# Low-rank scaling and key rotation moved into the attention, and the w_up block sums spread over 18 of its 24 items

## The chip, the cores and the metric

The kernel runs on one core of one Trainium2 chip. The metric is the device time of one execution in microseconds (us), given as the median of three runs. Of the core's engines, PE (TensorE) multiplies matrices, DVE (VectorE), ACT (ScalarE) and POOL (GpSimd) work element by element, and SP only issues DMAs. POOL issues DMAs too; these are the only ones here that add to their destination.

## The reference

Two layers, each with a mixer of three parts that read one normalised input, then a memory cross-attention and a gated feed-forward network (FFN). What the change touches is the mixer's latent attention and the weights of the FFN:

```python
c_q, c_kv, k_rope, g_q, g_k, g_v, g_m = jnp.split(z, offs, axis=-1)          # 256, 128, 32 columns, ...
qa  = (rms_norm(c_q, mla_q_norm) @ mla_w_uq).reshape(B, S, MLA_HEADS, MLA_NOPE + MLA_ROPE)
kva = (rms_norm(c_kv, mla_kv_norm) @ mla_w_ukv).reshape(B, S, MLA_HEADS, MLA_NOPE + MLA_V)
k_pe = apply_rope(k_rope.reshape(B, S, 1, MLA_ROPE), *rope_a)
...
y_a = block_attention(q_a, k_a, v_a, (MLA_NOPE + MLA_ROPE) ** -0.5)          # 6 heads
y_b = block_attention(q_b, k_b, v_b, GQA_DIM ** -0.5)                        # 6 heads
...
a = h @ w_up                                                                 # 1024 x 5632, in the FFN
```

All is float32, with 1024 tokens and a width of 1024.

## The kernel before

A float32 product is made of three products of rounded halves (`mm3`, lines 115 to 118: hi·hi, hi·lo, lo·hi). So each operand is split: ACT writes the rounded half (lines 123 and 126), DVE the rest (lines 124 and 127).

The FFN multiplies 2 x 2 blocks by a seven-product scheme, which needs sums of blocks of `w_up`. They are made in DRAM while the attention runs: the class `Blocks` cuts `w_up` into 24 steps per layer (`steps`). Each step is a copy from DRAM to DRAM (`copy`, line 778, issued by SP) and later an adding DMA onto the copy (`add`, line 783, issued by POOL). Most of them move 1 MB. The sums of `w_down` have 12 copies in the same stretch; their adds come in the FFN.

The attention (`attention`) runs over 24 items, 12 of six heads with 64 columns (`gqa`), then 12 of the latent heads (`mla`), each item one head and half of the queries. An item has four steps: PE makes 1024 scores per row (lines 726 and 727 or `mm3`), DVE takes their maximum (line 295), ACT the exponentials (line 299), DVE the reciprocal of their sum (line 304) and POOL scales the row (line 305). Five steps later PE transposes the rows (line 140), ACT and DVE split them, and PE multiplies them with the values (lines 318 and 319); ACT and POOL put the two halves of a result together (lines 326 to 328).

Between the steps the attention runs what the lists `fill[item]` hold. `q_cols` (`fill[0]` and `fill[1]`) makes the latent queries from the transposed low-rank columns `cqT` (made by `turn_cq`) and the halves of `w_uq`; `rope_q(h)` (`fill[8 + 2h]`) rotates a head's queries: two DVE products (lines 236, 238), two POOL products (lines 237, 239), two DVE sums (lines 240, 241). `y_squares` adds squares on POOL (line 664). What `extra[item]` holds is run at the third step of an item: there stand the copies and adds.

Just ahead of the attention, the loop over `w_a` makes the low-rank columns in eight token tiles. Behind tiles 3 and 7 it scales a half of them by the reciprocal root of their mean squares (lines 551 to 556: two small DVE instructions, one on POOL, and two DVE products of 1024 and 512 columns). Behind the loop stands the rotation of the key columns `kr` (`rope`).

All this is recorded in program order, and a scheduler then sets each engine's order. Engines run their own queue in order and wait for each other by semaphores. The issue of an add is an entry of POOL's queue like any other, so what stands behind it waits for it.

The two lines that place a step n of 24 are:

```python
g = n * 14 // len(steps)
extra.setdefault(g + 4, []).append(lambda w=w, m=m, i=i: w.add(m, i))
```

Of the kernel before, what the change touches and what calls it, by code (L numbers as in the profile page):

```python
# [8 lines left out]
F32 = mybir.dt.float32  # L9
F32R = mybir.dt.float32r  # L10
AF = mybir.ActivationFunctionType
ALU = mybir.AluOpType
AX = mybir.AxisListType

P = 128
# [4 lines left out]
CH = 512  # L20
NC = S // CH
TPC = CH // P
# [47 lines left out]
def trunk(ctx: ExitStack, tc: tile.TileContext, a: dict, out: bass.AP):  # L70
# [16 lines left out]
    def stat():  # L87
        return stats.tile([P, 16], F32, tag="stat", name="stat")
# [7 lines left out]
    def v3(ap, b):  # L96
        return ap.rearrange("p (a b) -> p a b", b=b)
# [286 lines left out]
    def layer(l, nt, w_m, last):  # L384
# [129 lines left out]
        def turn_q(j, c):  # L514
# [7 lines left out]
            if c == 1:  # L522
                sl.put(zq[j])

        cq = [sl.get(F32) for _ in range(2)]
        ckv = sl.get(F32)
        kr = lpool.tile([P, NT * ROPE], F32, tag="kr", name="kr")
        for t in range(NT):
            b = proj(t, w_a, 416, 2)
            c, tt = divmod(t, TPC)  # L530
            if tt == 0:
                ssq = stat()
            junk = sl.get(F32)
            nc.scalar.activation(junk[:, :256], b[:, :256], AF.Square, accum_out=ssq[:, tt : tt + 1])
            nc.scalar.activation(junk[:, :P], b[:, 256:384], AF.Square, accum_out=ssq[:, 4 + tt : 5 + tt])
            sl.put(junk)
            nc.scalar.activation(cq[c][:, tt * 256 : (tt + 1) * 256], b[:, :256], AF.Copy)
            nc.scalar.activation(ckv[:, t * P : (t + 1) * P], b[:, 256:384], AF.Copy)
            nc.scalar.activation(kr[:, t * ROPE : (t + 1) * ROPE], b[:, 384:416], AF.Copy)
            if t == 0:  # L540
                qn_ = [head_norm(z, tab[:, T_GQ : T_GQ + 64], tab) for z in zq]
            for j, st in Q_STEPS[t]:
                qn_[j][st]()
            if t == 5:
                tc.keep_in_program_order(nc.scalar.activation(stat()[:, 0:1], mhalf[:, 0:1], AF.Exp))
            if t == 6:
                turn_q(0, 0)
                turn_q(0, 1)
            if tt == TPC - 1:
                v, r = stat(), stat()  # L550
                nc.vector.tensor_scalar(v[:, 0:4], ssq[:, 0:4], 1.0 / 256, EPS, ALU.mult, ALU.add)
                nc.vector.tensor_scalar(v[:, 4:8], ssq[:, 4:8], 1.0 / P, EPS, ALU.mult, ALU.add)
                nc.gpsimd.tensor_tensor(r[:, :8], v[:, :8], mhalf[:, :8], ALU.pow)
                for z, n, o in ((cq[c], 256, 0), (ckv[:, c * CH : (c + 1) * CH], P, 4)):
                    z = v3(z, n)
                    nc.vector.tensor_tensor(z, z, r[:, o : o + 4].unsqueeze(2).to_broadcast([P, TPC, n]), ALU.mult)
        put2(w_a)
        nt.free()
        w_uq = [load(a["w_uq"][l, k], 576, True) for k in range(2)]
        w_ukv = load(a["w_ukv"][l], 768, True)  # L560
        cos3, sin3 = v3(tab[:, T_COSA : T_COSA + P], 16), v3(tab[:, T_SINA : T_SINA + P], 16)
        tmp = sl.get(F32)
        rope(kr.rearrange("p (t i two) -> p t i two", i=16, two=2), cos3, sin3, [v3(tmp[:, o * P : (o + 1) * P], 16) for o in range(4)])
        sl.put(tmp)


        cqT, ckvT, kT, qn, vm, qT, yT = [None] * 2, [None], [None] * 3, [None] * MLA_H, {}, {}, [None] * KT
# [229 lines left out]

        items = [gqa(h, c) for h in range(GQA_H) for c in range(NC)]
        items += [mla(h, c) for h in range(MLA_H) for c in range(NC)]
        fill[0] += [lambda k=k: turn_cq(0, k) for k in range(2)]  # L800
        fill[1] += [lambda k=k: turn_cq(1, k) for k in range(2)]
        for t in range(NT):
            fill[t // 4] += [lambda t=t: q_cols(t, 0), lambda t=t: q_cols(t, 1)]
# [46 lines left out]

        extra, steps = {}, w_u.steps()
        for n, (w, m, i) in enumerate(steps):
            g = n * 14 // len(steps)
            extra.setdefault(g, []).append(lambda w=w, m=m, i=i: w.copy(m, i))
            extra.setdefault(g + 4, []).append(lambda w=w, m=m, i=i: w.add(m, i))
        later = deque(sorted(w_d.steps(), key=lambda s: (5, 7, 6, 3).index(s[1])))
        for n, (w, m, i) in enumerate(later):
            extra.setdefault(n * 20 // len(later), []).append(lambda w=w, m=m, i=i: w.copy(m, i))
# [624 lines left out]
```

## Time and profile before

| what | us |
|---|---|
| median of three runs (2798.71 to 2804.17) | 2800.31 |
| the profiled execution | 2792.72 |
| its span, first to last instruction | 2790.7 |
| PE busy in the span | 2732.1 |
| DVE, ACT, POOL busy | 1966.8, 1469.7, 688.0 |

The profile is of one execution. A row of its timeline is: start in us, length in us, engine, line, operation, what is written and read, and in brackets how long the engine had been idle before and what is taken to have released it. "PEclk" or "granted clock" is the share of TensorE's full clock.

### The profile page before, as it was taken

The page shows a single profiled execution, that of the slowest core. Times are in us where ns is not written, and L with a number is a line of the kernel's source. Part 1 is how long each engine was busy: PE and PEld are TensorE (multiplying, and loading weights), DVE is VectorE, ACT ScalarE, POOL GpSimd, SP SyncE. Part 2 cuts the span into 40 slices and gives each one's busy share as a digit, 9 for nine tenths or more (in the row PEclk, how much of TensorE's full clock was granted, in tenths as well). Part 3 has the DMA queues.
Part 4 walks back from the last instruction along what each step waited for, and adds up shares of the span by engine and source line. Part 5 has one row for each costly group of instructions (what it writes and reads, how often), then busy time and mean ns, then how long its engine had stood idle before and what let it go on. Part 6 is the DMA issues. An engine that isn't in the chain of part 4 may idle for free.

```text
span 2790.7 us, 37974 instructions
## 1 busy us (share of the span) xinstructions
PE 2732.1 (98%) x13648; PEld 2289.4 (82%) x13648; DVE 1966.8 (70%) x2953; ACT 1469.7 (53%) x2838; POOL 688.0 (25%) x696
## 2 busy tenths in 40 slices
PE   9999999999999999999999999999999999999998
PEld 7987778888878888888889877788888788888887
DVE  5489889666697777774445798895566877777754
ACT  4368878324564444553333788782245544446442
POOL 3245666320001100000123355653200011100000
PEclk9999999999999999999999999999999999999999
DMA  4028991221149876785210389912211698757752
GB/s 145 27 80 229 264 243 38 79 65 48 65 138 237 227 211 169 223 270 185 86 59 21 108 244 251 226 39 68 69 61 46 165 242 221 205 173 233 257 184 104
DMA packets 160748, 418.80 MB, mean 150 GB/s; under 512 B 17840, under 2 KB 18480, under 8 KB 146224
## 3 DMA queue, kind: packets, MB, share of 16 engines
q1 hardware_dynamic: 137376, 323.84, 34.3%
q0 software_dynamic: 23040, 92.28, 18.1%
q8 instruction: 107, 1.75, 0.2%
q14 instruction: 81, 0.66, 0.1%
q10 hardware_dynamic: 144, 0.26, 0.0%
HBM read 371.75 MB, written 206.05 MB: 207 GB/s over the span
## 4 chain that ended last, share of the span: by engine, by line
PE 84%; DVE 6%; ACT 4%; issue 2%; POOL 2%; DMA 1%; SPq 0%; POOLq 0%; DVEq 0%; ACTq 0%
PE bank L1237 8%; PE bank L116 7%; PE bank L118 7%; PE bank L117 7%; PE pair L1237 6%; PE bank L140 6%; PE bank L1125 5%; PE bank L1126 5%; PE bank L1124 5%; PE pair L1124 4%; PE pair L1125 4%; PE pair L1126 4%; PE pair L116 2%; PE pair L118 2%; PE pair L117 2%; PE bank L319 2%
## 5 line engine op out<-in xcount | busy, mean ns | idle before, releaser
L116 PE MATMUL bank<-s,s 128*128 128x512 f32 (+4 forms) x1124 | 405.1, 360 | 5.6 <-DVE s L124 3.8
L124 DVE TENSOR_TENSOR s<-bank,s 128x512 fp32r<-128x512 f32 (+3 forms) x552 | 330.8, 630 | 106.1 <-ACT s L123 103.4
L118 PE MATMUL bank<-s,s 128*128 128x512 f32 (+4 forms) x1124 | 400.0, 357 | 5.4 <-DVE s L127 4.2
L117 PE MATMUL bank<-s,s 128*128 128x512 f32 (+4 forms) x1124 | 399.0, 355 | 0.3 <-DVE s L111 0.3
L123 ACT ACTIVATE s<-bank 128x512 fp32r<-128x512 f32 (+3 forms) x552 | 286.3, 556 | 208.9 <-PE bank L140 138.0
L140 PE MATMUL bank<-ident,s 128*128 128x128 f32 (+1 forms) x2320 | 327.8, 275 | 22.8 <-ACT s L327 6.4
L140 PEld LDWEIGHTS bank<-ident,s 128*128 128x128 f32 (+1 forms) x2320 | 272.4, 140 | 84.2 <-ACT s L327 12.2
L1077 ACT ACTIVATE s<-s 128x512 fp32r<-128x512 f32 x308 | 187.4, 627 | 181.5 <-PE bank L1126 46.6
L305 POOL TENSOR_SCALAR s<-s,stat 128x1024 f32<-128x1024 f32 x192 | 224.5, 1176 | 217.1 <-DVE stat L304 152.9
L1125 PE MATMUL bank<-s,s 128*128 128x512 f32 x704 | 274.5, 390 | 0.9 <-DVE s L209 0.9
L1126 PE MATMUL bank<-s,s 128*128 128x512 f32 x704 | 273.9, 389 | 0.0
L1124 PE MATMUL bank<-s,s 128*128 128x512 f32 x704 | 273.8, 389 | 0.0
L295 DVE TENSOR_REDUCE stat<-pair 128x1 f32<-128x1024 f32 x192 | 233.8, 1218 | 45.9 <-PE pair L727 27.1
L1237 PE MATMUL bank<-s,s 128*128 128x512 f32 (+1 forms) x1068 | 242.6, 387 | 1.6 <-DVE stat L131 1.6
L116 PEld LDWEIGHTS bank<-s,s 128*128 128x128 f32 x1124 | 212.4, 189 | 33.9 <-DVE s L124 5.6
L132 POOL TENSOR_TENSOR stat<-stat,mhalf 128x1 f32<-128x1 f32 (+3 forms) x94 | 82.2, 875 | 634.7 <-DVE stat L131 633.1
L118 PEld LDWEIGHTS bank<-s,s 128*128 128x128 f32 x1124 | 212.3, 189 | 31.1 <-DVE s L127 5.1
L1222 DVE TENSOR_TENSOR s<-s,s 128x512 fp32r<-128x512 f32 x264 | 170.8, 686 | 93.5 <-ACT s L1221 93.5
L1237 PEld LDWEIGHTS bank<-s,s 128*128 128x128 f32 x1068 | 198.7, 188 | 42.3 <-DVE x L1328 1.8
L117 PEld LDWEIGHTS bank<-s,s 128*128 128x128 f32 x1124 | 212.6, 189 | 23.8 <-DVE s L111 0.6
L299 ACT ACTIVATE s<-pair,stat 128x1024 f32<-128x1024 f32 x192 | 214.9, 1119 | 26.1 <-DVE stat L295 22.1
L1221 ACT ACTIVATE s<-s 128x512 fp32r<-128x512 f32 x264 | 153.7, 623 | 141.8 <-DMA s<-g_u 49.6
(182 smaller groups left out, 5529.2 us busy)
## 6 DMA issues: line engine op xcount, KB each, us to landing
s<-u SPq DMA_DIRECT2D x176, 256.0 KB, 4.2
u<-in_w_up SPq DMA_DIRECT2D x40, 1024.0 KB, 17.9
s<-in_w_up SPq DMA_DIRECT2D x132, 256.0 KB, 4.4
g_u<-s SPq DMA_DIRECT2D x88, 256.0 KB, 2.8
s<-g_u SPq DMA_DIRECT2D x88, 256.0 KB, 3.2
s<-d SPq DMA_DIRECT2D x88, 256.0 KB, 3.5
u<-in_w_up POOLq DMA_DIRECT2D x20, 1024.0 KB, 21.1
u<-u POOLq DMA_DIRECT2D x20, 1024.0 KB, 15.9
```

The lines of the kernel that those rows point to most:

```text
L116: nc.tensor.matmul(o, l[0], r[0], start=first, stop=False)
L117: nc.tensor.matmul(o, l[0], r[1], start=False, stop=False)
L118: nc.tensor.matmul(o, l[1], r[0], start=False, stop=last)
L123: nc.scalar.activation(hi, src, AF.Copy)
L124: nc.vector.tensor_tensor(lo, src, f(hi), ALU.subtract)
L140: nc.tensor.transpose(b[:m, j * P : (j + 1) * P], s, ident)
L295: nc.vector.reduce_max(self.nm[:, 0:1], s, axis=AX.X, negate=True)
L305: Item.last = nc.gpsimd.tensor_scalar(p, p, r[:, 0:1], 0.0, ALU.mult, ALU.add)
L1124: nc.tensor.matmul(o, lh, rh, start=k == 0 and m in (1, 5, 6), stop=False, skip_group_check=True)
L1125: nc.tensor.matmul(o, lh, rl, start=False, stop=False, skip_group_check=True)
L1126: nc.tensor.matmul(o, ll, rh, start=False, stop=k == 3, skip_group_check=True)
L1237: nc.tensor.matmul(o, lh[p], rh[q], start=m in (1, 5, 2) and i == 0 and k == 0, stop=i == NP - 1 and k == 2, skip_group_check=True)
```

## The change

It does three things. The scaling of the low-rank columns becomes a function `norm_low`; its second call (tiles 4 to 7) moves from the end of the projection to `fill[0]`, behind the transposes of the first half. The rotation of the keys becomes `rope_k` and moves to `fill[4]`. The 24 steps of `w_up` are put on 18 items in place of 14, and each add three items behind its copy in place of four: copies in items 0 to 17 in place of 0 to 13, adds in items 3 to 20 in place of 4 to 17. What is computed stays the same.

```diff
+        def norm_low(c, ssq):
+            v, r = stat(), stat()
+            nc.vector.tensor_scalar(v[:, 0:4], ssq[:, 0:4], 1.0 / 256, EPS, ALU.mult, ALU.add)
+            nc.vector.tensor_scalar(v[:, 4:8], ssq[:, 4:8], 1.0 / P, EPS, ALU.mult, ALU.add)
+            nc.gpsimd.tensor_tensor(r[:, :8], v[:, :8], mhalf[:, :8], ALU.pow)
+            for z, n, o in ((cq[c], 256, 0), (ckv[:, c * CH : (c + 1) * CH], P, 4)):
+                z = v3(z, n)
+                nc.vector.tensor_tensor(z, z, r[:, o : o + 4].unsqueeze(2).to_broadcast([P, TPC, n]), ALU.mult)
...
-            if tt == TPC - 1:
...
+            if t == TPC - 1:
+                norm_low(0, ssq)
...
-        tmp = sl.get(F32)
-        rope(kr.rearrange("p (t i two) -> p t i two", i=16, two=2), cos3, sin3, [v3(tmp[:, o * P : (o + 1) * P], 16) for o in range(4)])
-        sl.put(tmp)
+
+        def rope_k():
+            tmp = sl.get(F32)
+            rope(kr.rearrange("p (t i two) -> p t i two", i=16, two=2), cos3, sin3, [v3(tmp[:, o * P : (o + 1) * P], 16) for o in range(4)])
+            sl.put(tmp)
...
-        fill[0] += [lambda k=k: turn_cq(0, k) for k in range(2)]
+        fill[0] += [lambda k=k: turn_cq(0, k) for k in range(2)] + [lambda: norm_low(1, ssq)]
+        fill[4] += [rope_k]
...
-            g = n * 14 // len(steps)
+            g = n * 18 // len(steps)
             extra.setdefault(g, []).append(lambda w=w, m=m, i=i: w.copy(m, i))
-            extra.setdefault(g + 4, []).append(lambda w=w, m=m, i=i: w.add(m, i))
+            extra.setdefault(g + 3, []).append(lambda w=w, m=m, i=i: w.add(m, i))
```

The diff does not show what the scheduler makes of it. The rows below are of the built programs, in each engine's own order; "waits" are the engines whose semaphores an instruction waits for. The added lines move line numbers: 551 to 556 become 527 to 532, 664 becomes 669, 783 becomes 788.

DVE at the start of the first layer's attention, before: the second scaling (lines 551, 552, 556) and the rotation of `kr` (236 to 241) stand between the first maximum (295) and the two splits of the transposed low-rank columns (127, of the banks), for which PE's `q_cols` waits.

```order
L551 TENSOR_SCALAR stat<-stat 128x4 [waits Activation_49]
L552 TENSOR_SCALAR stat<-stat 128x4 [waits Activation_49]
L295 TENSOR_REDUCE stat<-pair 128x1 [waits PE_49]
L556 TENSOR_TENSOR s_102_1255<-s_102_1255,stat 128x1024 [waits Activation_49,Pool_49]
L556 TENSOR_TENSOR s_103_1256<-s_103_1256,stat 128x512 [waits Activation_49]
L236 TENSOR_TENSOR s_132_1616<-kr,s_73_703 128x128 [waits Activation_49]
L111 TENSOR_TENSOR s_128_1606<-s_126_1604,s_127_1605 128x576 [waits DMAHW7_49,DVE_49,Activation_49]
L238 TENSOR_TENSOR s_132_1616<-kr,s_73_703 128x128
L127 SCALAR_TENSOR_TENSOR s_135_1670<-bank,cols_86,s_134_1669 128x512 [waits PE_49]
L240 TENSOR_TENSOR kr<-s_132_1616 128x128 [waits DVE_49,Pool_49]
L241 TENSOR_TENSOR kr<-s_132_1616 128x128 [waits Pool_49]
L127 SCALAR_TENSOR_TENSOR s_137_1679<-bank,cols_86,s_136_1678 128x512 [waits PE_49]
```

The same place in the changed kernel:

```order
L295 TENSOR_REDUCE stat<-pair 128x1 [waits PE_49]
L127 SCALAR_TENSOR_TENSOR s_134_1656<-bank,cols_86,s_133_1655 128x512 [waits Activation_49]
L127 SCALAR_TENSOR_TENSOR s_136_1665<-bank,cols_86,s_135_1664 128x512 [waits Activation_49]
L527 TENSOR_SCALAR stat<-stat 128x4
L528 TENSOR_SCALAR stat<-stat 128x4
L295 TENSOR_REDUCE stat<-pair 128x1 [waits PE_49]
L111 TENSOR_TENSOR s_128_1599<-s_126_1597,s_127_1598 128x576 [waits DMAHW7_49,DVE_49,Activation_49]
L532 TENSOR_TENSOR s_102_1255<-s_102_1255,stat 128x1024 [waits Pool_49]
L532 TENSOR_TENSOR s_103_1256<-s_103_1256,stat 128x512
```

The two splits now stand right behind the first maximum, and the scaling behind them, with the second maximum ahead of its products; the rotation is gone from here.

POOL around the rotation of the fourth latent head (item 14), before: two adds in a row, then row scalings (305), a sum of squares (664) and the rotation's two products.

```order
L783 DMA u_5_4_1627<-in_w_up 128x2048 [waits DMAHW6_49]
L783 DMA u_5_5_1628<-in_w_up 128x2048 [waits DMAHW7_49]
L305 TENSOR_SCALAR s_340_3884<-s_340_3884,stat 128x1024 [waits DVE_49,Activation_49]
L664 TENSOR_TENSOR s_318_3683<-s_318_3683,s_344_3936 128x1024
L305 TENSOR_SCALAR s_343_3930<-s_343_3930,stat 128x1024 [waits DVE_49,PE_49]
L237 TENSOR_TENSOR s_348_3974<-s_142_1712,s_73_703 128x128 [waits PE_49]
L239 TENSOR_TENSOR s_348_3974<-s_142_1712,s_73_703 128x128
```

The same place in the changed kernel:

```order
L788 DMA u_3_2_1629<-u_6_2_1617 128x2048 [waits DMAHW4_49,DMASW6_49,DMASW3_49]
L305 TENSOR_SCALAR s_340_3877<-s_340_3877,stat 128x1024 [waits DVE_49,Activation_49]
L669 TENSOR_TENSOR s_318_3676<-s_318_3676,s_344_3928 128x1024 [waits Activation_49]
L237 TENSOR_TENSOR s_348_3966<-s_141_1705,s_73_703 128x128 [waits PE_49]
L239 TENSOR_TENSOR s_348_3966<-s_141_1705,s_73_703 128x128
L305 TENSOR_SCALAR s_343_3922<-s_343_3922,stat 128x1024 [waits DVE_49]
```

One add stands there in place of two, an earlier one in the order of the steps (5_4 and 5_5 now come some twenty entries later), and the rotation's products stand directly behind the sum of squares.

DVE at the place that the rotation of `kr` is moved to, some three items into the attention, in the changed kernel (before, lines 124, 295 and 304 follow each other here without it):

```order
L304 RECIPROCAL stat<-stat 128x1 [waits Activation_49]
L124 TENSOR_TENSOR s_189_2345<-bank,s_189_2345 128x512 [waits DVE_49,Activation_49]
L124 TENSOR_TENSOR s_190_2353<-bank,s_190_2353 128x512 [waits DVE_49,Activation_49]
L236 TENSOR_TENSOR s_192_2362<-kr,s_73_703 128x128 [waits DVE_49]
L238 TENSOR_TENSOR s_192_2362<-kr,s_73_703 128x128
L295 TENSOR_REDUCE stat<-pair 128x1 [waits PE_49]
L240 TENSOR_TENSOR kr<-s_192_2362 128x128 [waits DVE_49,Pool_49]
L241 TENSOR_TENSOR kr<-s_192_2362 128x128 [waits Pool_49]
```

The four DVE instructions of the rotation now stand between splits and maxima of the attention, where POOL is scaling rows. The second layer has the same orders.

## Rows read from the trace of the kernel before

**Rows 1.** Page, part 1: busy us, share of span, instructions of each engine.
```profile
PE 2732.1 (98%) x13648; PEld 2289.4 (82%) x13648; DVE 1966.8 (70%) x2953; ACT 1469.7 (53%) x2838; POOL 688.0 (25%) x696
```
**Rows 2.** Timeline, DVE, start of the first layer's attention: start, length, engine, line.
```profile
166.03 1.23 DVE L295 TENSOR_REDUCE stat<-pair 128x1 f32<-128x1024 f32 x1
167.74 2.35 DVE L556 TENSOR_TENSOR s<-s,stat 128x1024 f32<-128x1024 f32 x2 [0.49 <-POOL stat L553]
...
170.22 0.74 DVE L111 TENSOR_TENSOR s<-s,s 128x576 fp32r<-128x576 f32 x1
...
171.09 0.74 DVE L127 SCALAR_TENSOR_TENSOR s<-bank,cols,s 128x512 fp32r<-128x512 f32 x1
```
**Rows 3.** Timeline, PE: at this start, and near the end of the rotations.
```profile
171.88 0.40 PE L118 MATMUL bank<-s,s 128*128 128x288 f32 x1 [2.11 <-DVE s L127]
...
412.16 0.63 PE L140 MATMUL bank<-ident,s 128*128 128x128 f32 x4 [0.97 <-DVE s L124]
```
**Rows 4.** Timeline, POOL, in three stretches (both layers), around adds (L783).
```profile
299.73 0.81 POOL L783 DMA_DIRECT2D u<-in_w_up  x1 [3.87 <-DVE s L124]
300.29 2.50 POOL L305 TENSOR_SCALAR s<-s,stat 128x1024 f32<-128x1024 f32 x2
302.48 0.73 POOL L237 TENSOR_TENSOR s<-s,s 128x128 f32<-128x128 f32 x1
...
357.02 0.81 POOL L783 DMA_DIRECT2D u<-in_w_up  x1 [2.44 <-DVE s L124]
...
358.68 2.67 POOL L664 TENSOR_TENSOR s<-s,s 128x1024 f32<-128x1024 f32 x1
...
1741.13 0.84 POOL L783 DMA_DIRECT2D u<-in_w_up  x1 [4.17 <-DVE stat L304]
```
**Rows 5.** DMA issues by line at 285.0 and at 340.6 us: KB, us to landing.
```profile
u<-u POOLq DMA_DIRECT2D x1, 1024.0 KB, 14.4
...
u<-in_w_up SPq DMA_DIRECT2D x1, 1024.0 KB, 43.9
```
**Rows 6.** Timeline, DVE and PE, in the same three stretches.
```profile
300.59 3.20 DVE L236 TENSOR_TENSOR s<-s,s 128x128 f32<-128x128 f32 x1
...
305.78 0.50 PE L319 MATMUL bank<-s,s 128*128 128x512 f32 x1 [2.13 <-DVE s L124]
...
359.83 3.60 DVE L236 TENSOR_TENSOR s<-s,s 128x128 f32<-128x128 f32 x1
...
366.55 0.66 PE L140 MATMUL bank<-ident,s 128*128 128x128 f32 x4 [2.66 <-ACT s L327]
...
1742.22 5.34 DVE L236 TENSOR_TENSOR s<-s,s 128x128 f32<-128x128 f32 x1
...
1746.61 0.44 PE L140 MATMUL bank<-ident,s 128*128 128x128 f32 x2 [1.26 <-POOL s L305]
...
1750.66 0.98 PE L140 MATMUL bank<-ident,s 128*128 128x128 f32 x4 [2.92 <-ACT s L327]
```
**Rows 7.** Line L236: count, duration ns min/median/max, first and last start.
```profile
L236 DVE TENSOR_TENSOR s<-s,s x12: 274/926/5337, 272.3 to 1795.3; 128x128 f32<-128x128 f32 x12
```
**Rows 8.** Windows: us, busy PE, PEld, DVE, ACT, POOL, granted clock, DMA share, GB/s.
```profile
307.00:310.40 3.40, 3.40 (x12) 2.75 (x12) 2.67 (x4) 3.29 (x7) 1.45 (x2) 0.50 1.05 260
1556.40:1559.60 3.20, 3.20 (x15) 3.20 (x14) 2.20 (x4) 2.64 (x13) 1.16 (x2) 0.50 0.00 0
...
175.00:232.00 57.00, 56.30 (x348) 47.95 (x347) 45.92 (x78) 51.74 (x129) 24.34 (x23) 1.00 0.43 144
232.00:425.00 193.00, 181.12 (x1010) 146.22 (x1009) 167.94 (x290) 157.03 (x317) 118.24 (x116) 0.99 1.00 252
```
**Rows 9.** DMA queues from 232 to 425 us: packets, MB, share of 16 engines.
```profile
q0 software_dynamic: 3456, 23.07, 61.8%
q1 hardware_dynamic: 3600, 25.43, 37.7%
```
**Rows 10.** Line L295 in 160 to 560 us: duration ns, first and last start.
```profile
L295 DVE TENSOR_REDUCE stat<-pair x96: 1199/1215/1226, 166.0 to 501.6; 128x1 f32<-128x1024 f32 x96
```

More of the change, by code (lines that the diff above doesn't have):

```diff
@@ L548, in layer @@
                 turn_q(0, 1)
-            if tt == TPC - 1:
[L550 to L556, printed above, removed]
+            if t == TPC - 1:
+                norm_low(0, ssq)
         put2(w_a)
```

## The prediction

> **What bounds the kernel now.** I read the page first, then the stretch of the attention, then its stalls one by one. PE is busy 98% of the span [rows 1], so a time can only be won where PE stands still or runs slowly. Outside the attention the change touches nothing. In the attention the windows show a PE that is mostly full, beside a DMA share of 1.00 for 193 us on end [rows 8]. The timeline then shows which stalls are long, and two kinds stand out.
>
> The first is at the start. PE stops for 2.11 us at a product of `q_cols` until DVE has split the transposed low-rank columns [rows 3]. DVE could have split them behind the first maximum, which ends at 167.26, but in its queue the products of the second scaling (2.35 us), a weight split (0.74) and two products of the key rotation come first, and the split starts at 171.09 [rows 2]. The second layer shows the same 2.11 us. [...]
>
> The second kind starts in POOL. Three times POOL stands idle for 3.87, 2.44 and 4.17 us directly before it issues an add [rows 4]. The release that the bracket names is that of the next row's scaling; what fits is the landing of an older add. The first wait ends at 299.73; an add issued at 285.0 lands 14.4 us later, at 299.4 [rows 5], and in each of the three cases three adds were on their way and the wait ended 0.3 us after the oldest landed. So a fourth add is not taken while three are under way. Behind the wait POOL works off its queue without a pause: scalings, the sum of squares, the rotation's products [rows 4]. DVE's first product of a rotation, which reads two tiles in SBUF, lasts 3.20, 3.60 and 5.34 us just there [rows 6], against a shortest of 274 ns [rows 7], and the first of them ends, at 303.79, only when POOL's run is over (its product of L237 ends at 303.21, and L239 follows directly). PE then stands for 2.13, for 2.66 and for 1.26 and 2.92 us [rows 6], and behind the first the clock is 0.50 for 3.4 us [rows 8]; there is another such drop near 1751 behind the last, and one near 1782 without a long stall. So three causes lie in a row: too many adds at once, a POOL that catches up, a DVE that is held.
>
> **The sum, part by part.** It is made against the profiled execution, 2792.7 us with 2 us outside its span. The median of the runs, 2800.3, lies 7.6 us above it; I carry the difference over to it unchanged. A difference of 0.2%, 5.6 us, is about what a measurement of this kernel can tell from none.
>
> *The scaling moved.* The built order puts both splits right behind the first maximum. They then end near 167.3 + 2 x 0.74 = 168.7, and PE comes to the waiting product at 171.88 - 2.11 = 169.8, so this wait is gone. What is late next is the second weight half (L111): behind the two small instructions and the second maximum (1.2 us [rows 10]) it ends near 171, and PE has a dozen products ahead that do not need it. The scaling's own 2.35 us are not saved but now lie beside PE's products; its result is needed a whole item later, and its POOL step meets a POOL that has nothing to scale yet. Bounds: 1.2 to 2.6 us won per layer (the second maximum, and so all that hangs on it, comes sooner too); I take the 2.1 of the row, so -4.2. The clock drop of the second layer at 1556 goes with it: half of 3.2 us, -1.6 (between 0 and -1.6).
>
> *The rotation of the keys moved.* Its four DVE instructions come off the same queue at the start, counted above. Three items on they stand beside a working POOL. Nothing in the trace shows them there, so the other rotations must serve: their first product takes 274 to 5337 ns, median 926 [rows 7]; behind one that was held for about 1.1 us PE lost 0.97 us [rows 3]. Bounds 0 to 0.97 per layer while no add makes POOL catch up; I take the middle, 0.5, so +1.0. The two POOL products are moved past adds too, but their reader, the transposes of the keys, comes three items later.
>
> *The adds spread.* An item takes (501.6 - 166.0) / 95 x 4 = 14.1 us [rows 10]. The DMA engines' work of this stretch is 0.43 x 57 + 1.00 x 193 = 218 us of all sixteen [rows 8], of which adds are 0.618 x 193 = 119 [rows 9]. Before, adds run from 231 to 425. In the changed kernel they start an item sooner and end three items later, about 217 to 467, and copies run some 254 us: 119 / 250 + 99 / 254 = 86% of the engines. So the backlog should not build up, an add should land in some 10 to 15 us, and with 24 adds in 18 items (one per 10.6 us, in place of one per 8.2) the fourth finds the first landed. The POOL waits go, and with them the stalls: 2.13 + 2.66 + 1.7 for the clock = -6.5 in the first layer, 1.26 + 2.92 + 1.6 = -5.8 in the second. A copy has 3 x 14.1 = 42 us before its add in place of 56. That is short of the 43.9 us that one took in the full stretch [rows 5], but the same backlog made that time.
>
> What comes back: the fourth rotation now stands on POOL directly behind the sum of squares, so that DVE's first product is likely held there in both layers. Bounds: 0 and 2.66 of the second stall; I take the 0.97 of the shorter hold, +2.0. And the last four adds now are issued in items 18 to 20 among POOL's scalings and splits of the results, 0.8 us each; PE feels little of it, +0.8 in all (0 to 3).
>
> Sum: -4.2 - 1.6 - 6.5 - 5.8 + 1.0 + 2.0 + 0.8 = -14.3. That is 2778.4 for a profiled execution and 2786 for the median. The scheduler also reorders neighbouring scalings and splits in this stretch, where stalls under 1 us stand now; I see no sign for these and allow 3 us either way.
>
> [...] Rows show a DVE product held over four POOL instructions on end: 3.20 us against two scalings and two products [rows 4, 6]. [...]
>
> **The rivals.**
>
> *A: the fourth add still waits.* Copies and adds may stay full if DMA costs in the trace hide idle time, or if pairs of adds fall together. Then only the start is won: -4.2 - 1.6 + 1.0 = -4.8, 2795.5. For it: the share of 1.00 says nothing of how much demand there is beyond. Against it: 86% by the sum.
>
> *B: POOL runs hold the rotations without any wait for an add.* POOL's run at the fourth rotation needs no add: sum of squares 2.67, then two products of about 0.7, by the order with nothing between. If DVE arrives at its start, it is held for nearly 4 us, like the 3.60 us with 2.66 us of PE and a clock drop behind it. That is 2 x (2.66 + 1.7 - 0.97) = 6.8 more: -7.5, 2792.8. For it: the new order. Against it: DVE has two splits to do between the reciprocal that starts POOL's scaling and its product, so that it comes late into the run.
>
> *C: slower, since copies come too late.* The add waits on POOL for its copy, and all scalings of the attention queue behind. It decides when copies take over 42 us: one took 43.9. If the DMA engines stay full, the last eight adds of a layer would wait some 1.5 us each, 24 us in both layers, and before, 6.3 us of POOL waits cost PE 6.5 us with the clock. So 24 us, less the 5.8 won at the start: +18, 2818. Against it: the demand is spread over a quarter more time.
>
> *D: it does nothing that can be seen.* The order shows all three moves, so this needs the gains to be given back by chance: within 3 us of 2800.
>
> **How the numbers follow.** Forecast 0.60, A 0.12, B 0.20, C 0.05, D 0.03. Of the forecast nearly all (0.57) lies beyond 5.6 us; of B two thirds (0.14), of A less than half (0.05). So faster 0.76, same 0.19, slower 0.05. The range reaches from the whole gain with the larger win at the start and 3 us of good order, about -23, to just past A: 2777 to 2798. C and half of D lie above it.
>
> **What would show it.** In the changed trace: no PE wait of 2 us at the start of either attention; the second scaling behind the splits; idle time of POOL directly before an add under 0.5 us; DMA share between 225 and 460 us under 1.00 and adds that land in under 18 us; the first products of rotations mostly under 1.1 us; the clock drops at 307, 1556 and 1751 gone. I am wrong in the forecast if POOL still waits before adds (A, or C if it is for copies), or if a rotation beside the sum of squares lasts over 2 us (B).

## The result and the profile after

The changed kernel takes 2771.34 us (median of four runs, 2769.15 to 2774.25), the kernel before 2799.84 in the same comparison: a ratio of 0.9897, 95% interval 0.9882 to 0.9912. A second comparison, in a session of the experiments, gave 2771.8 against 2796.4, ratio 0.9907 (0.9884 to 0.9929). The forecast was 2786 with a range of 2777 to 2798: the direction was right, the gain twice as large as forecast, and the time lies below the range.

The profiled execution of the changed kernel took 2771.84 us, its span is 2770.1. PE does the same work in a shorter span, DVE is busy 14.6 us less than in [rows 1]:

```profile
PE 2730.2 (99%) x13648; PEld 2287.5 (83%) x13648; DVE 1952.2 (70%) x2953; ACT 1470.2 (53%) x2838; POOL 686.8 (25%) x696
```

The two attentions tell where the time went. The windows view was cut from the first score to the last product with the values of each layer (before 164.2 to 532.7 and 1547.4 to 1918.8 us, after 163.8 to 522.5 and 1536.5 to 1895.2). Its last line sums both windows: their length, then the busy time of each engine. First the kernel before, then the changed one:

```profile
sum 739.90, PE 707.28 PEld 582.65 DVE 628.61 ACT 574.95 POOL 408.59; mean PE 353.64 PEld 291.33 DVE 314.30 ACT 287.48 POOL 204.30
```

```profile
sum 717.40, PE 702.41 PEld 578.70 DVE 614.37 ACT 574.64 POOL 408.03; mean PE 351.20 PEld 289.35 DVE 307.18 ACT 287.32 POOL 204.01
```

The sums are read as two terms. Length less PE's busy time is PE's idle time: 739.90 - 707.28 = 32.6 us before, 717.40 - 702.41 = 15.0 after, so 17.6 us. PE's busy time itself falls by 4.9 us for the same products, which is what products cost that no longer run at half the clock: in the attentions the granted clock is 0.50 in four stretches of 3.4 us before (from 307, 1556, 1751 and 1782), in one after (from 387). Together 22.5 us. Outside the attentions the profiled execution loses 1.9 us: two stretches of clock 0.50, 3.4 us each, stand there at 1984 and 2148 that were not there before, and the one ahead of the first attention is 3.4 us shorter. So the span is 20.6 us shorter. The medians are 28.5 us apart; the difference of 7.9 us has its own section below.

At the start of the attention (DVE's timeline, as [rows 2]) the two splits now follow the first maximum, the scaling comes behind the second maximum and the weight half, and PE has no wait there:

```profile
165.37 1.23 DVE L295 TENSOR_REDUCE stat<-pair 128x1 f32<-128x1024 f32 x1
166.51 1.40 DVE L127 SCALAR_TENSOR_TENSOR s<-bank,cols,s 128x512 fp32r<-128x512 f32 x2
...
169.10 0.75 DVE L111 TENSOR_TENSOR s<-s,s 128x576 fp32r<-128x576 f32 x1
169.81 1.83 DVE L532 TENSOR_TENSOR s<-s,stat 128x1024 f32<-128x1024 f32 x2
```

In POOL's timeline two adds in a row are issued with no bracket, thus without a wait, and the rotation behind them (L237) starts 0.1 us after DVE's product, not in a run of held work as in [rows 4, 6]:

```profile
293.42 1.65 POOL L788 DMA_DIRECT2D u<-in_w_up  x2
...
297.53 0.52 POOL L237 TENSOR_TENSOR s<-s,s 128x128 f32<-128x128 f32 x1
```

All first products of the rotations together (as [rows 7]), the time from an add's issue to its landing in the first layer, and the window of the copies and adds (as [rows 8]; the DMA share, 0.86, is the number before the last):

```profile
L236 DVE TENSOR_TENSOR s<-s,s x12: 273/280/345, 273.4 to 1773.5; 128x128 f32<-128x128 f32 x12
```

```profile
DMA to landing us min/median/max: 7.8/13.5/21.7
```

```profile
225.00:460.00 235.00, 229.85 (x1295) 187.63 (x1294) 205.04 (x364) 198.78 (x398) 144.18 (x140) 0.99 0.86 221
```

The longest of these products fell from 5337 to 345 ns. One long stall is left in each layer, 1.46 us in the first, behind the fourth rotation. POOL, DVE and PE there:

```profile
348.24 1.12 POOL L305 TENSOR_SCALAR s<-s,stat 128x1024 f32<-128x1024 f32 x1 [2.25 <-DVE stat L304]
349.34 2.40 POOL L669 TENSOR_TENSOR s<-s,s 128x1024 f32<-128x1024 f32 x1
351.71 0.46 POOL L237 TENSOR_TENSOR s<-s,s 128x128 f32<-128x128 f32 x1
...
352.63 1.27 POOL L305 TENSOR_SCALAR s<-s,stat 128x1024 f32<-128x1024 f32 x1
```

```profile
349.17 0.32 DVE L236 TENSOR_TENSOR s<-s,s 128x128 f32<-128x128 f32 x1
```

```profile
353.95 0.77 PE L140 MATMUL bank<-ident,s 128*128 128x128 f32 x5 [1.46 <-POOL s L305]
```

DVE's product is not held here. The row's scaling at 352.63 is what comes late: it stands in POOL's queue behind 2.40 us of squares and two rotation products.

Last, who made PE wait in 175 to 520 us, before and after (rows of 0.2 us left out): what is waited for, then the total in us, how many waits, the longest.

```profile
PE bank L140 <- ACT s L327: 2.9, 2, 2.7
PE bank L140 <- DVE s L124: 2.5, 6, 1.0
PE bank L319 <- DVE s L124: 2.1, 1, 2.1
PE bank L140 <- POOL s L305: 1.9, 2, 1.0
PE pair L726 <- ACT s L299: 1.5, 3, 0.7
PE bank L318 <- DVE s L124: 0.9, 1, 0.9
PE bank L116 <- DVE s L124: 0.9, 1, 0.9
...
```

```profile
PE bank L140 <- POOL s L305: 2.3, 2, 1.5
PE bank L140 <- ACT s L327: 1.3, 4, 0.4
PE bank L140 <- DVE s L124: 1.1, 4, 0.4
PE bank L116 <- DVE s L124: 0.7, 1, 0.7
PE pair L731 <- ACT s L299: 0.7, 2, 0.5
...
```

Two of the rows of before are the long stalls of the forecast (2.7 and 2.1 us). The others are many waits of up to 1.0 us, and those shrank too: this the forecast did not have.

### The profile page after: what moved, and what is told of

It is laid out like the page before. It is cut to its first block, busy times and chain, and to the rows that moved or that the text cites. A ratio compares the mean times of both kernels' runs of the same rounds, so it can differ in the third digit from the quotient of the medians.

```text
span 2770.1 us, 37935 instructions
## 1 busy us (share of the span) xinstructions
PE 2730.2 (99%) x13648; PEld 2287.5 (83%) x13648; DVE 1952.2 (70%) x2953; ACT 1470.2 (53%) x2838; POOL 686.8 (25%) x696
## 4 chain that ended last, share of the span: by engine, by line
PE 88%; DVE 4%; ACT 4%; POOL 2%; DMA 1%; issue 1%; SPq 0%; POOLq 0%; DVEq 0%; ACTq 0%
PE bank L1243 8%; PE bank L116 7%; PE bank L118 7%; PE bank L117 7%; PE bank L140 7%; PE pair L1243 6%; PE bank L1131 5%; PE bank L1132 5%; PE bank L1130 5%; PE pair L1130 4%; PE pair L1131 4%; PE pair L1132 4%; PE bank L318 3%; PE bank L319 3%; PE pair L116 2%; PE pair L118 2%
## 5 line engine op out<-in xcount | busy, mean ns | idle before, releaser
L116 PE MATMUL bank<-s,s 128*128 128x512 f32 (+4 forms) x1124 | 404.6, 361 | 4.5 <-DVE s L124 3.4
L124 DVE TENSOR_TENSOR s<-bank,s 128x512 fp32r<-128x512 f32 (+3 forms) x552 | 330.8, 629 | 108.4 <-ACT s L123 105.5
L295 DVE TENSOR_REDUCE stat<-pair 128x1 f32<-128x1024 f32 x192 | 233.6, 1217 | 39.1 <-PE pair L118 19.0
L116 PEld LDWEIGHTS bank<-s,s 128*128 128x128 f32 x1124 | 212.0, 189 | 33.5 <-DVE s L124 3.8
L1228 DVE TENSOR_TENSOR s<-s,s 128x512 fp32r<-128x512 f32 x264 | 170.7, 685 | 95.8 <-ACT s L1227 94.2
L117 PEld LDWEIGHTS bank<-s,s 128*128 128x128 f32 x1124 | 212.5, 189 | 24.2 <-DVE s L111 0.6
L1084 DVE TENSOR_TENSOR s<-s,s 128x512 fp32r<-128x512 f32 x308 | 202.0, 686 | 33.8 <-ACT s L1083 31.1
## 6 DMA issues: line engine op xcount, KB each, us to landing
u<-in_w_up SPq DMA_DIRECT2D x40, 1024.0 KB, 13.5
```

The source lines that it names most:

```text
L116: nc.tensor.matmul(o, l[0], r[0], start=first, stop=False)
L117: nc.tensor.matmul(o, l[0], r[1], start=False, stop=False)
L124: nc.vector.tensor_tensor(lo, src, f(hi), ALU.subtract)
L295: nc.vector.reduce_max(self.nm[:, 0:1], s, axis=AX.X, negate=True)
```

## Experiments

All times are medians; the kernel before, run beside them, had 2797.3, 2796.4 and 2797.5 us in the three sessions. The first two sessions ran on one chip; the third, with the rotation back, the small adds and the two other places for the adds, ran on another. "Idle" is always PE's idle time in both attentions together, from the sum of the windows as above: 32.6 us before, 15.0 after.

### Does the fourth add wait for room, and does PE's stall hang on it?

Before, with `dynamic_dma_scratch_size` at 1472 in place of 1024 and every instruction in its old place on every engine. The expectations call it room for descriptors; that it holds these is the author's reading, and the runs show only what its size does:

```diff
-    nc = _bacc.Bacc("TRN2", target_bir_lowering=False, num_devices=1, dynamic_dma_scratch_size=1024)
+    nc = _bacc.Bacc("TRN2", target_bir_lowering=False, num_devices=1, dynamic_dma_scratch_size=1472)
```

> [...] Theory R: the fourth add waits for room for its descriptors, which the oldest of the three frees when it lands. Then with 1.44 times the room a fourth is taken at once: the waits of 3.87, 2.44 and 4.17 us go, POOL doesn't catch up, the first products of the rotations there take about 0.3 to 1 us, and the time falls by 5 us to 20 us (the stalls that I laid to these waits are 2.13 and 2.66 us in one layer and 1.26 and 2.92 in the other, with the clock 12.3 us). Rival N: the limit is a number of adds or the full DMA engines; then the waits stay and the time is within 3 us of before. If the waits go but PE's stalls stay, the chain of causes from POOL's wait to PE is wrong.

It took 2786.5 us, ratio 0.9964 (0.9951 to 0.9977): 10 us faster. POOL's timeline at the first and second place of [rows 4], DVE's and the line of all first products:

```profile
296.03 1.68 POOL L783 DMA_DIRECT2D u<-in_w_up  x2
298.84 1.12 POOL L305 TENSOR_SCALAR s<-s,stat 128x1024 f32<-128x1024 f32 x1 [1.13 <-DVE stat L304]
...
356.31 2.40 POOL L664 TENSOR_TENSOR s<-s,s 128x1024 f32<-128x1024 f32 x1
358.70 1.28 POOL L305 TENSOR_SCALAR s<-s,stat 128x1024 f32<-128x1024 f32 x1
359.95 0.46 POOL L237 TENSOR_TENSOR s<-s,s 128x128 f32<-128x128 f32 x1
```

```profile
301.57 0.93 DVE L236 TENSOR_TENSOR s<-s,s 128x128 f32<-128x128 f32 x1
...
358.54 0.32 DVE L236 TENSOR_TENSOR s<-s,s 128x128 f32<-128x128 f32 x1
```

```profile
L236 DVE TENSOR_TENSOR s<-s,s x12: 273/332/1079, 273.2 to 1787.0; 128x128 f32<-128x128 f32 x12
```

```profile
sum 732.30, PE 706.52 PEld 581.74 DVE 619.46 ACT 575.96 POOL 409.63; mean PE 353.26 PEld 290.87 DVE 309.73 ACT 287.98 POOL 204.81
```

The fourth add is issued at once, with three under way, at each of the four places where that happens (before, it waited 3.87, 2.44, 1.90 and 4.17 us). The products of 3.20, 3.60 and 5.34 us now take 0.93, 0.32 and 0.33, and PE's stalls of 2.13, 2.66, 1.26 and 2.92 us are gone. Since nothing else differs between the programs, the whole chain (no room, POOL waits, POOL catches up, DVE is held, PE stands) is shown as a whole, not only argued; how POOL holds DVE is looked at in the last section. It is worth 10 us, where the forecast had 12.3 with the clock. Idle falls from 32.6 to 25.8 us: of the 8.97 us of stalls some 2 come back in other waits. The many short ones stay, nearly to the same length (0.88, 0.94 and 1.00 us at three places before, 0.89, 0.96 and 1.00 here), so they belong to the program, by its order or its traffic, and not to one execution; and idle is still 10.8 us above that of the changed kernel.

The same memory for the changed kernel:

> [...] Theory R: with the adds spread, never more than three are under way, so that the larger memory has nothing to give: within 3 us of the changed kernel. If it is 5 us faster or more, the changed kernel still waits for room somewhere.

It took 2771.7 us, the changed kernel beside it 2771.8. Nothing waits for room any more, and theory R holds on this side too.

### Which part of the change brings what?

The adds alone (against the kernel before):

```diff
-            g = n * 14 // len(steps)
+            g = n * 18 // len(steps)
...
-            extra.setdefault(g + 4, []).append(lambda w=w, m=m, i=i: w.add(m, i))
+            extra.setdefault(g + 3, []).append(lambda w=w, m=m, i=i: w.add(m, i))
```

> The adds spread as in the change (18 items, three behind the copy), the scaling and the key rotation left where they were. By my steps the start of the attention keeps its 2.11 us wait in both layers, and the clock drop at 1556: this kernel wins what the changed one wins, 28.5 us, less 5.8, so about -23. Rival M: the moves are worth more than the wait that they end, since they also take six DVE instructions out of a crowded start; then -15 to -18 here.

The two moves alone (against the changed kernel the same two lines, undone):

```diff
-            g = n * 18 // len(steps)
+            g = n * 14 // len(steps)
...
-            extra.setdefault(g + 3, []).append(lambda w=w, m=m, i=i: w.add(m, i))
+            extra.setdefault(g + 4, []).append(lambda w=w, m=m, i=i: w.add(m, i))
```

> The scaling and the key rotation moved as in the change, the adds left on 14 items, four behind the copy. By my steps -5.8 at the start, and up to +1.0 for the rotation beside a working POOL: 2794 to 2795. POOL's waits before adds and the held rotations behind them stay. Rival M (as for the adds alone): -10 or more.

The whole once more, on the same chip:

> The changed kernel, beside the adds alone (-14.5 us by its ratio) and the moves alone (-7.0) on the same chip. If the two parts only add up, it stands at -21.5, some 2776 here. If they gain from each other, as the first measurement (-28.5) says, it stands at 2768 to 2771, and the 7 us are to be found as PE's gaps of the attention that each part alone still has: the adds alone have 12.2 and 12.4 us of gaps in the two attentions, the moves alone 16.9 and 14.9, the changed kernel 6.9 and 7.9.

The adds alone took 2781.8 us, ratio 0.9948 (0.9933 to 0.9963), about -14.5. The moves alone took 2790.4, ratio 0.9975 (0.9964 to 0.9986), about -7. The whole took 2771.8, ratio 0.9907, about -25. So the adds alone fall short of my -23, as rival M said. But M also wanted -10 or more of the moves alone, and these stand near the -5.8 of my steps: neither account holds for both. The whole is some 3 to 4 us better than the sum of the parts; that difference is within the intervals of the ratios, but idle says the same: 24.8 us (726.70 - 701.91) with the adds alone and 29.4 (735.90 - 706.49) with the moves alone, 7.8 and 3.2 won; together they would leave 21.6, and 15.0 to 16.0 were found.

With the moves alone POOL waits as before, and PE's stall at the fourth rotation stays:

```profile
295.72 0.82 POOL L788 DMA_DIRECT2D u<-in_w_up  x1 [3.05 <-DVE stat L304]
...
353.49 0.82 POOL L788 DMA_DIRECT2D u<-in_w_up  x1 [3.25 <-DVE s L124]
```

```profile
363.00 1.11 PE L140 MATMUL bank<-ident,s 128*128 128x128 f32 x4 [2.90 <-ACT s L327]
```

To see which move gains from the spread adds, the rotation went back to its old place in the changed kernel:

```diff
+        rope_k()
...
-        fill[4] += [rope_k]
```

> The changed kernel with the key rotation back at the end of the projection; the scaling stays moved. In DVE's order the rotation's first two products stand ahead of the splits again (0.28 us each in the trace of the adds alone) and the sums between them. By my steps the front wait of PE comes back in part, at most 4 x 0.2 to 0.3 = 0.8 to 1.1 us per layer, and the rotation beside a working POOL, which I priced at 0.5 per layer, is saved: within 2 us of the changed kernel. If it is 4 us or more slower, the rotation's move is what makes the two parts of the change gain from each other, by the order that it leads to.

It took 2778.4 us, ratio 0.9934 (0.9915 to 0.9953): 6.6 us slower than the changed kernel's 2771.8 of the other session and chip, where I had put 2 at most; the intervals of the two ratios overlap. The front wait comes back small, 0.52 and 0.59 us. Idle is 19.6 us (722.80 - 703.19) against 15.0 to 16.0, and the longest waits that the changed kernel does not have are 1.16, 1.13 and 0.51 us, in items 4, 7 and 9. The first two in the list of PE's waits, 175 to 520 us:

```profile
PE bank L140 <- DVE s L124: 3.0, 5, 1.1
...
PE bank L116 <- ACT s L327: 1.2, 1, 1.2
```

The adds alone, which have the rotation at the same old place, show the same row of L116 (1.2, 1, 1.2) and the same 1.1 us at L124; the order on the engines differs between these two kernels only at the start of the attentions (165 to 180 and 1545 to 1559 us). So these waits go with the built order: the rotation at item 4 puts other work between the maxima there, and behind it the small splits of the latent keys and their products stand at other places. Which of these entries ends them is not shown. The move that I priced as a cost of 1.0 us is worth some 4 us of idle time in this order, 6.6 by the medians; the moved scaling, by the adds alone against this kernel, 5.2 of idle time (24.8 and 19.6), 3.4 by the medians (2781.8 and 2778.4).

### What do the adds cost besides the waits?

Without the adds (against the kernel before):

```diff
-            extra.setdefault(g + 4, []).append(lambda w=w, m=m, i=i: w.add(m, i))
```

> The kernel before without the 24 adds of a layer in the attention (the sums are left out, the copies stay). It bounds what the adds cost in their old places: POOL doesn't issue them or wait, and 119 us of the DMA engines' work is gone. If the waits for room are all that they cost PE, it stands where the larger descriptor memory stands, at 2784 to 2788. If the mere issue (0.56 to 0.79 us of POOL for each) and the traffic cost as well, it is some 5 us or more below that.

With all adds issued, but small:

```diff
-                tc.keep_in_program_order(nc.gpsimd.dma_start(self.sum[m, i], src, accum_op=ALU.add))
+                tc.keep_in_program_order(nc.gpsimd.dma_start(self.sum[m, i][:, :16], src[:, :16], accum_op=ALU.add))
```

> The kernel before with every add of the attention cut to 16 of its columns (the sums come out incomplete): the issues stay in POOL's order, nothing of them waits for room, and their 119 us of DMA work are gone. The kernel without adds won 24.6 us, the one with more room for descriptors 10.8. Theory I: what lies between them is traffic or the issues. If it is the traffic, it goes here too: 2770 to 2774. If it is the issues, it stays: 2784 to 2788. Theory O: it is the order that the scheduler builds, in which DVE, ACT and PE pass short gaps to each other; then the gaps of 0.4 to 1.0 us stay wherever the order is that of before, and go where it differs (from the sixth item on some products and splits change places): between the two, 2776 to 2782.

Both leave the sums of `w_up` out or incomplete, so only their times count. They took 2771.7 us, ratio 0.9912 (0.9892 to 0.9932), and 2773.5, ratio 0.9920 (0.9905 to 0.9935). Their sums:

```profile
sum 715.80, PE 700.55 PEld 584.83 DVE 613.65 ACT 575.26 POOL 369.89; mean PE 350.28 PEld 292.41 DVE 306.83 ACT 287.63 POOL 184.95
```

```profile
sum 722.40, PE 701.31 PEld 583.27 DVE 622.62 ACT 575.92 POOL 409.37; mean PE 350.65 PEld 291.64 DVE 311.31 ACT 287.96 POOL 204.68
```

So the adds in their old places cost 24.6 us, of which waits for room are 10. In the attentions the two kernels have one order on every engine but for the issues themselves, so what lies between them there is the issues and the little that they move: 5.9 us of idle time (21.1 against 15.3). By the medians it is 1.8 us, but the edit cuts the adds of `w_down` in the FFN too. The issues are at most a part of the rest. Whether the larger part is the traffic or the built order these two kernels don't tell, because the scheduler, for which the size of an add counts, built an order for both that differs from the one before from about the sixth item on. The time speaks for the traffic (inside 2770 to 2774). The next kernels speak against it: they carry all of the traffic and are faster, by the medians, than the one without any add.

### Other places for the adds

The changed kernel with the adds four items behind (first line pair), and with 20 items and three behind (second):

```diff
-            extra.setdefault(g + 3, []).append(lambda w=w, m=m, i=i: w.add(m, i))
+            extra.setdefault(g + 4, []).append(lambda w=w, m=m, i=i: w.add(m, i))
```

```diff
-            g = n * 18 // len(steps)
+            g = n * 20 // len(steps)
```

> The changed kernel with the adds four items behind their copies in place of three. In the changed kernel no add waits for its copy, so by my theory the distance gives and takes nothing: 2769 to 2775, and the adds end an item later. Rival C's root, copies that come late, would be seen as a gain here; more than 3 us of loss would say that the adds' place late in the attention costs, or that another built order has other gaps.

> The changed kernel with the adds on 20 items in place of 18: still fewer under way. Since the changed kernel shows no wait before any add, more spread has nothing of that kind to win: 2769 to 2775 by theory R. The last adds then stand in item 22, nearer the end of the attention, which can cost up to 3 us by my bound for the late adds.

Four items behind: 2764.6 us (2761.8 to 2767.5), ratio 0.9886 (0.9871 to 0.9902). Twenty items: 2768.0 (2766.9 to 2772.9), ratio 0.9902 (0.9885 to 0.9918). I had expected 2769 to 2775 of both: the first lies 4 us below, the second 1. By medians the first beats both kernels, the changed one by 7 us, the second by 3 to 4; the intervals of the ratios overlap, but idle says the same:

```profile
sum 712.00, PE 701.09 PEld 581.39 DVE 614.55 ACT 574.76 POOL 406.55; mean PE 350.55 PEld 290.69 DVE 307.27 ACT 287.38 POOL 203.28
```

```profile
sum 714.30, PE 702.28 PEld 577.91 DVE 616.98 ACT 573.35 POOL 409.88; mean PE 351.14 PEld 288.95 DVE 308.49 ACT 286.68 POOL 204.94
```

That is 10.9 and 12.0 us. No add of the changed kernel waited for its copy, so late copies (the root of rival C) are not what is cured. What is left is the order, of which one piece can be seen. At the fourth rotation of the first layer the sum of squares starts 2.6 us earlier than in the changed kernel, a row's scaling stands between it and the rotation's products, and the stall of 1.46 us is gone:

```profile
346.77 2.39 POOL L669 TENSOR_TENSOR s<-s,s 128x1024 f32<-128x1024 f32 x1
...
349.15 1.28 POOL L305 TENSOR_SCALAR s<-s,stat 128x1024 f32<-128x1024 f32 x1
...
350.39 0.47 POOL L237 TENSOR_TENSOR s<-s,s 128x128 f32<-128x128 f32 x1
```

Both kernels have the whole traffic and less idle time than the kernel without adds (15.3 us), though in the order of neither was a kernel without adds run. So the traffic as such need not cost PE anything; a traffic that costs only in the old order is not excluded.

### Why the medians are further apart than the profiles

> The kernel before, unchanged. Its profiled execution took 2792.7 us, while its timed runs took 2798.7 to 2804.2; the changed kernel shows no such difference. Theory S: the stalls of the attention differ from one execution to the next, and the profiled one had few of them. Then a profile of a run near 2799 has attentions (first scores to last value product) longer than 368.5 and 371.4 us, by some 7 us together, with more POOL waits before adds than the three of rows 4, or longer ones. Rival W: the 7 us lie elsewhere (the start, the FFN, the clock). Then the attentions stay within 1 us of 368.5 and 371.4. The ratio is 1.000 by both.

> The kernel before once more, for a second profiled execution: on this chip its runs spread from 2790.9 to 2808.0 us with a median of 2797.3, and the one whose trace I read, 2792.7, is among the fastest. Theory S: an execution near the median has more stall in the attentions than 368.5 and 371.4 us hold, by some 5 us together. Rival W: the attentions stay within 1 us of these, and the difference lies in the start or in the clock elsewhere.

The first took 2797.7 us (ratio 1.0004, 0.9995 to 1.0014); its profiled execution, of 7029.9 us, says nothing of these stalls. The second gave a profiled execution of 2795.1 us. Its sum over the attentions:

```profile
sum 742.20, PE 709.53 PEld 584.07 DVE 627.72 ACT 575.78 POOL 410.38; mean PE 354.76 PEld 292.03 DVE 313.86 ACT 287.89 POOL 205.19
```

The attentions are 2.3 us longer, 370.5 and 371.7 us. Theory S fails as I put it: PE's idle time is the same in sum, 32.7 against 32.6 us (single stalls differ by up to 0.5). Rival W fails as I put it too, since the first attention is 2.0 us longer, but the clock, which it named, is what differs: PE's busy time is 709.53 against 707.28 for the same products, and the clock is 0.50 for 3.4 us at 172.8 and at 367.4 us, where the first execution has 1.00. The mean granted clock of the two executions is 0.995 and 0.996. Over all runs of the kernel before that carry a mean granted clock it is 0.994 to 0.997, mostly 0.995; in the eight runs of the changed kernel it is 0.997 to 0.999, in the middle between 0.997 and 0.998. At half the clock PE takes nearly twice the time (in the stretch of clock 0.50 of the kernel before, 307.0 to 310.4 us, products of 512 columns start 0.43 us apart, at full clock 0.23), so the time lost is at most (1 - clock) x span: about 14 us at 0.995, 7 at 0.9975. The profiled pair, 0.996 and 0.997, has 11 and 8 us. So the medians are further apart than the profiles by about 4 us from the clock; as the clock is given to 0.001, thus to 1.4 us, this explains about half of the 7.9 us. The rest stays open, but a second pair hardly shows it: the spans of the second profile of the kernel before and of the second of the changed one are 2793.3 and 2769.8, 23.5 us apart, and the medians of that session 24.6. So the first profile of the kernel before was a fast execution, and its first comparison (2799.84) lay 2.3 to 3.5 us above the three later medians.

## Why the prediction was wrong, point by point

**What bounds the kernel, and the three causes in a row: right.** PE's stalls vanished with POOL's waits, both in the changed kernel and with nothing changed but `dynamic_dma_scratch_size`. I overlooked a fourth wait of the kind, 1.90 us before an add at 1682.51 us; the product of the rotation behind it took 0.92 us, and PE did not stand there, so a wait of POOL alone does not tell what it costs.

**The scaling moved: right.** The 2.11 us wait is gone in both layers, -4.2 as forecast, and nothing is late next.

**The adds spread: right in the mechanism.** The DMA share is 0.86, as summed (86%). Adds land after 13.5 us in the median (10 to 15 forecast), pairs after up to 21.7, over the 18 that I named. No add waits, and no first product of a rotation is held. Stalls of 8.97 us are gone; at the fourth rotation 1.46 and 1.47 came, 2.93 against 2.0 forecast. That the term is near is luck, since I gave the wrong reason: DVE is not held there, a row's scaling is late in POOL's queue.

**The clock: right in size by luck, wrong as a rule.** I let three drops to 0.50 go with their stalls, -4.9 in all, and PE's busy time in the attentions fell by 4.9. But four went and one came there, and in the second pair of profiles it fell by 8.1 (709.53 to 701.41). Drops came elsewhere (387, 1984, 2148), with no stall over 1.03 us in the 6 us ahead. So in these executions they follow no single stall.

**The short waits: the step that failed.** "I see no sign for these and allow 3 us either way" was the term for stalls under 1 us. Of 17.6 us less idle, 4.2 are the start and 6.0 the held rotations (8.97 - 2.93). The other 7.4 are these waits, for which my sum had +1.8 (the key rotation and the late adds). So this term was off by 9 us, and one give-back had the wrong sign: the moved key rotation, +1.0 by forecast, is worth -4 to -7 beside the spread adds. I had priced the rotation's own duration (it took 0.33 us, with no hold) and not the order that forms around it. For the rotation's move, which leaves the adds where they are, it is the order that matters; whether the spread adds shorten waits by the order or by the traffic, and which entry of the order makes each wait, stays open.

**Carrying 7.6 us over unchanged: failed too.** The two kernels' runs differ in clock by more than the two profiled executions do. With -20.6 in place of -14.3 I would still have forecast 2780, inside the range; by this pair of profiles it is the carry that put the time below it. By the second pair, -23.5, the forecast would have been 2776.8, at the range's end, so the split between the two failed steps is known to some 3 us only.

**The rivals.** A falls: no add waits. B falls: the run of POOL at the fourth rotation exists and costs 1.46 us, but without a hold; it lasts 3.3 us (349.34 to 352.65) and not nearly 4, because the rows whose lengths I added overlap. C falls: no add waits for its copy, and in the first layer copies landed after 24.2 us at most, where they have 42. (The copy of 43.9 us in [rows 5] was issued at 1736 us, in the second layer, and not at 340.6; the slowest of the first layer took 43.7.) D falls by the result.

## What to carry to other kernels

Where a full engine is fed by three others in an order that a scheduler builds, list the many short waits as a group with their sum, not only the long stalls: a change that moves work there can rebuild the order, so a good part of the gain (here 7.4 of 17.6 us of idle time) may lie in waits too short to stand out. Where an adding DMA stops the queue that issues it while earlier ones are under way (here the fourth of 1 MB, for 1.90 to 4.17 us), look for what stands directly behind it in that queue; a larger `dynamic_dma_scratch_size` was a cheap test for it here (10 us at 1472 in place of 1024). Profile the same kernel twice before carrying the distance between a profile and a median over to another kernel.

## What the runs showed of the hardware

A DVE product of two SBUF tiles lasted across several POOL instructions on end, not only across the one that ran at its start. The 128x128 product took 0.28 us alone (before, at 388.23 us), 0.93 when it met one POOL scaling a third of the way through (with the larger memory, at 301.57), and 3.20, 3.60 and 5.34 across four or five instructions (before, [rows 6]). That POOL works without a pause was not enough for this: with the larger memory it works through from 355.22 to 362.09 us, and the product at 358.54, near the end of the squares, takes 0.32. In the traces of the kernel before and of the changed one a product of a rotation outlasted more than one POOL instruction only where these stand behind an add with no idle time between. There, in the kernel before, a row starts about 0.3 us before the one ahead has ended, the add's included (299.73 to 302.48 in [rows 4]); behind an idle time the rows overlap by 0.03 in the median. With the adds alone the longest first product took 1.66 us. Why the rows overlap, and whether the overlap is what keeps DVE out, is not shown.

POOL itself was not slowed in such a run, though its rows look longer (2.67 us in place of 2.40 for the squares). Its instructions start 1.09, 2.38, 1.09 and 0.42 us apart from 357.59 us on in the kernel before, and 1.09, 2.39, 1.25 and 0.42 from 355.22 on with the larger memory, where DVE is not held.

The granted clock was not set by the program alone. The same two stretches of the changed kernel, in its two profiled executions (columns as above; the clock is the third number from the end):

```profile
380.10:386.90 6.80, 6.80 (x45) 5.89 (x44) 3.49 (x10) 5.48 (x13) 4.55 (x5) 1.00 1.02 240
386.90:390.30 3.40, 3.18 (x12) 2.40 (x11) 3.00 (x6) 1.63 (x3) 1.88 (x3) 0.50 1.08 277
...
771.40:774.80 3.40, 2.79 (x11) 2.00 (x12) 3.40 (x7) 1.15 (x2) 0.00 (x0) 1.00 0.00 0
```

```profile
380.10:386.90 6.80, 6.80 (x45) 5.89 (x44) 3.44 (x10) 5.41 (x13) 4.63 (x5) 1.00 1.02 237
386.90:390.30 3.40, 2.78 (x15) 2.00 (x14) 3.07 (x7) 1.75 (x3) 1.89 (x3) 1.00 1.06 272
...
771.40:774.80 3.40, 3.39 (x8) 2.20 (x9) 3.31 (x6) 1.15 (x2) 0.00 (x0) 0.50 0.00 0
```

At 386.9 PE had been busy for all of 6.8 us in both executions, and the clock fell to 0.50 in the first alone; at 771.4 it fell to 0.50 in the second alone.
